# Tracing both score matmuls of a pair of token tiles ahead of VectorE's reads of the scores

## The chip, the cores and the metric

The kernel runs on one core of one Trainium2 chip. The metric is device time in microseconds (us) of one execution, from the first instruction to the last with what the launch adds around them. Engines are named as the profile names them: PE is TensorE's matmuls, PEld its weight loads, DVE is VectorE, ACT is ScalarE, POOL is GpSimd, and SP (SyncE) issues most of the DMAs.

## What is computed

The reference is one inference step of a two-layer decoder trunk: one layer of dilated-window attention (three groups of eight heads), one RG-LRU recurrent layer. There is a prompt of 1024 tokens and, beside it, eight sequences with eight new tokens each that attend to caches in HBM ("decode" below). For the prompt the part that the change touches is, per head:

```python
s = jnp.einsum('brnqhd,brnkhd->brnhqk', qb, kk) * (HEAD_DIM ** -0.5) + bias
lse = jax.nn.logsumexp(s, axis=-1)
p = jnp.exp(s - lse[..., None])
o = jnp.einsum('brnhqk,brnkhd->brnqhd', p, vv)
```

A block of 128 queries sees its own block of 128 keys and, in the groups with window 128 and 512, the block before it.

## The kernel before

All of it is fp32. The weight matmuls split each operand into a high and a low part and run three matmuls for one (lines 132, 133, 134; lines 140 and 141 for the eight sequences), each with 384 columns.

**Stages.** After a start of some 60 us, `attention_phase` runs 24 heads in the group order 1, 2, 0. A head has four quarters. Each quarter makes Q, K and V of two token tiles (`qkv_head`), normalises Q and K and transposes them on TensorE through the PSUM tile `ptq` (line 486), from which ACT copies QT (line 487) and ACT or DVE copies KT (lines 489, 491). Then it takes one attention pair from a queue that is three quarters behind (`next_att`, `att_part`, `att_pair`). From head 8 on, pieces of the decode of the caches are put between the quarters (`background`): cache tiles `kv` are loaded by SP, multiplied on POOL, DVE or ACT (lines 793, 841, 836, 829) and summed on DVE and ACT (lines 803, 798, 846), and two matmuls at line 856 close each decode. After the heads come the output projection and the recurrent layer, in which there are no pairs.

**One pair.** `att_pair` works on two token tiles, t = 0 and 1. The scores of both go into the two halves of one PSUM tile `ps_s` (line 322); there is one such buffer. DVE reads a tile's scores, adds the bias, writes `s_sb` and takes the row's extreme into `ob` (line 323, and a second small instruction that reads the accumulator); ACT takes the exponential (line 325). TensorE transposes the result into the PSUM tile `pt` (line 329), which uses the same single buffer as `ptq`. A copy to `pT` (line 94 or 92), the product with V (line 336) and a copy of the result follow. In the last group the result tile is `o3`, freed by the store `GTd<-o` and filled by loads `o<-Od`.

**What sets the order.** The program is traced in the order of the Python code. A scheduler then gives each engine its own list, which that engine executes strictly in order, and puts independent work (the weight matmuls above all) between dependent steps. Dependencies are kept by whole tiles: in the code before, the score matmul of t = 1 writes the tile that DVE's read of t = 0 reads, so it waits for that read although the halves differ.

Of the kernel before, what the change touches and what calls it, by code (L numbers as in the profile page):

```python
# [74 lines left out]
class Trunk:  # L75
# [231 lines left out]
    def att_pair(self, g, h, j, QT, KT, V, bt, ob):  # L307

        nc = self.nc
        kbs = []  # L310
        for t in range(2):
            i = 2 * j + t
            prev = [[i - 1], [i - 4], []][g]
            kbs.append([q for q in prev if q >= 0] + [i])
        ps = self.ps_s.tile([128, 2, 256], F32, name="ps_s", tag="s")
        pt = self.ps_t.tile([128, 4, 128], F32, name="pt", tag="t")
        po = self.ps_o.tile([128, 2, 132], F32, name="ps_o", tag="o")
        sb = self.p_a.tile([128, 2, 256], F32, name="s_sb", tag="s_sb", bufs=2)
        for t, kb in enumerate(kbs):
            nk = 128 * len(kb)  # L320
            kv = KT[:, kb[0], :] if len(kb) == 1 else KT[:, kb[0]:kb[1] + 1:kb[1] - kb[0], :]
            nc.tensor.matmul(ps[:, t, :nk], lhsT=QT[:, 2 * j + t, :], rhs=kv, start=True, stop=True)  # L322
            nc.vector.tensor_tensor_reduce(out=sb[:, t, :nk], in0=ps[:, t, :nk], in1=bt[:, 256 - nk:], scale=-1.0,  # L323
                                           scalar=3e38, op0=OP.add, op1=OP.min, accum_out=ob[:, t, 129:130])
            nc.scalar.activation(sb[:, t, :nk], sb[:, t, :nk], AF.Exp, bias=ob[:, t, 129:130], scale=-1.0)
        n = 0
        for t, kb in enumerate(kbs):
            for q in range(len(kb)):
                nc.tensor.transpose(pt[:, n, :], sb[:, t, 128 * q:128 * q + 128], self.ident)  # L329
                n += 1  # L330
        pT = self.p_a.tile([128, 4, 128], F32, name="pT", tag="pT", bufs=2)
        self.evac(pT[:, :n], pt[:, :n])
        n = 0
        for t, kb in enumerate(kbs):
            for q, b in enumerate(kb):
                nc.tensor.matmul(po[:, t, :129], lhsT=pT[:, n, :], rhs=V[:, b, :129],  # L336
                                 start=(q == 0), stop=(q == len(kb) - 1))
                n += 1
        self.evac(ob[:, :, :129], po[:, :, :129])
# [954 lines left out]
```

## Time and profile before

| | before |
|---|---|
| three runs, us | 1994.94, 1998.83, 1994.72 (median 1994.94) |
| profiled execution, us | 1996.83 |
| its span, first to last instruction, us | 1994.90 |
| busy, us | PE 1823.5, PEld 1748.5, DVE 1182.4, ACT 978.4, POOL 647.2 |

The page shows shares over the whole span. Because the stages have different limits, the rows below are mostly from single stretches: heads without decode (60 to 430 us), the first decode (430 to 804), the change to the last group and the second decode (804 to 1165), and heads with little decode (1165 to 1460). "a <- b: total, times, longest" in a list of waits means that a stood idle until b was done.

### The profile page before, as it was taken

To read this page: it belongs to the slowest core of one execution; us is meant where nothing else is said; L and a number is where in the kernel's file an instruction comes from. 1 tells how busy PE (TensorE), PEld (TensorE's weight loads), DVE (VectorE), ACT (ScalarE), POOL (GpSimd) and SP (SyncE) were. 2 spreads that over 40 slices of the span, in tenths; PEclk is the share of its full clock that TensorE was granted. 3 is DMA by queue.
4 is the path that set the end of the run, shared out by engine and by line. 5 is a ranking of instruction groups with operands and counts; after the bars stand their busy time and mean duration, and the time that the engine had idled before them with its cause. 6 is when DMAs were issued, how large, how long until landed. Compare 5 with 4: busy or idle time off the path is not lost.

```text
span 1994.9 us, 31531 instructions
## 1 busy us (share of the span) xinstructions
PE 1823.5 (91%) x11152; PEld 1748.5 (88%) x11152; DVE 1182.4 (59%) x2339; ACT 978.4 (49%) x3025; POOL 647.2 (32%) x606
## 2 busy tenths in 40 slices
PE   7999999978888767978887799999999999999998
PEld 7999999978888666977877689999999899999998
DVE  6334333459874999546658755455566667767721
ACT  5544444638776666442234445455423346666510
POOL 4101111247673998239746521020100000001300
PEclk9999999989999887988998899999999999999999
DMA  6655657556766656546756654454575256643231
GB/s 203 193 184 186 197 160 224 161 166 200 208 191 181 183 155 183 146 146 220 222 173 190 212 166 137 161 160 120 182 257 176 83 195 218 215 155 118 83 122 62
DMA packets 261518, 344.01 MB, mean 172 GB/s; under 512 B 19644, under 2 KB 229888, under 8 KB 259312
## 3 DMA queue, kind: packets, MB, share of 16 engines
q1 hardware_dynamic: 253540, 228.38, 39.2%
q10 hardware_dynamic: 7820, 113.61, 16.3%
q8 instruction: 88, 1.44, 0.3%
q14 instruction: 70, 0.57, 0.1%
HBM read 296.20 MB, written 157.93 MB: 228 GB/s over the span
## 4 chain that ended last, share of the span: by engine, by line
PE 47%; DMA 17%; DVE 12%; POOL 8%; ACT 7%; issue 6%; SPq 2%; ACTq 0%; DVEq 0%; POOLq 0%
PE ps_g L134 8%; PE ps_g L133 8%; PE ps_g L132 8%; POOL pr L841 4%; DMA kv<-in_cache_kv_w_dram 4%; DMA wraw<-in_rnn_w_in_dram 3%; DMA wraw<-in_attn_w_in_dram 3%; PE ps_o L336 2%; PE ps_s L322 2%; PE ps_g L1180 2%; PE ps_g L1179 2%; PE ps_g L1178 2%; POOL pr L793 2%; DVE xn L475 1%; PE ps_g L1053 1%
## 5 line engine op out<-in xcount | busy, mean ns | idle before, releaser
L132 PE MATMUL ps_g<-w,xt 128*128 128x384 f32 (+1 forms) x1920 | 668.6, 351 | 19.6 <-DVE th L400 12.2
L133 PE MATMUL ps_g<-w,xt 128*128 128x384 f32 (+1 forms) x1920 | 665.0, 347 | 3.0 <-DVE w L99 1.7
L134 PE MATMUL ps_g<-w,xt 128*128 128x384 f32 (+1 forms) x1920 | 663.8, 346 | 0.0
L132 PEld LDWEIGHTS ps_g<-w,xt 128*128 128x128 f32 x1920 | 371.9, 194 | 25.9 <-DVE th L400 13.8
L133 PEld LDWEIGHTS ps_g<-w,xt 128*128 128x128 f32 x1920 | 372.2, 194 | 7.6 <-POOL w L118 2.1
L134 PEld LDWEIGHTS ps_g<-w,xt 128*128 128x128 f32 x1920 | 371.6, 194 | 1.7
L164 POOL TENSOR_TENSOR rs<-ms,mhalf 128x4 f32<-128x4 f32 (+2 forms) x138 | 138.3, 1004 | 624.4 <-DVE ms L162 607.1
L841 POOL TENSOR_TENSOR pr<-kv,ds 128x512 f32<-128x512 f32 x116 | 182.9, 1604 | 45.1 <-DVE acc L846 17.6
L793 POOL TENSOR_TENSOR pr<-kv,dq 128x512 f32<-128x512 f32 x118 | 168.0, 1453 | 87.0 <-DMA dq<-sd 42.3
L846 DVE TENSOR_TENSOR acc<-acc,pr 128x1024 f32<-128x1024 f32 x89 | 139.7, 1590 | 11.2 <-POOL pr L841 10.9
L323 DVE CUSTOM_DVE_ANT_0 s_sb<-ps_s,bias 128x128 f32<-128x128 f32 (+1 forms) x192 | 66.4, 346 | 118.3 <-PE ps_s L322 94.1
L322 PE MATMUL ps_s<-KT,QT 128*128 128x128 f32 (+1 forms) x384 | 99.1, 341 | 37.7 <-DVE o_sb L323 25.1
L462 ACT COPY xn<-ps_g 128x256 f32<-128x256 f32 x192 | 72.1, 375 | 120.3 <-PE ps_g L134 104.4
L466 ACT ACTIVATE sqj<-xn 128x128 bf16<-128x128 f32 x384 | 121.2, 316 | 10.4 <-issue 5.2
L99 DVE TENSOR_TENSOR w<-wraw,w 128x768 fp32r<-128x768 f32 (+1 forms) x88 | 83.5, 952 | 63.7 <-ACT w L98 63.3
L98 ACT CAST w<-wraw 128x768 fp32r<-128x768 f32 (+1 forms) x88 | 69.3, 804 | 100.4 <-DMA wraw<-in_attn_w_in_dram 51.0
L836 ACT ACTIVATE pr<-kv,ds 128x128 f32<-128x128 f32 x248 | 76.8, 391 | 72.5 <-DVE acc L846 37.8
L94 DVE COPY pT<-pt 128x256 f32<-128x256 f32 (+2 forms) x96 | 52.0, 541 | 97.0 <-PE pt L329 96.5
L803 DVE TENSOR_REDUCE ds<-pr 128x8 f32<-128x1024 f32 x73 | 88.1, 1213 | 33.1 <-POOL pr L793 33.0
L475 DVE SCALAR_TENSOR_TENSOR xn<-xn,rs,kg 128x128 f32<-128x128 f32 x192 | 94.2, 530 | 22.3 <-POOL rs L164 22.2
L322 PEld LDWEIGHTS ps_s<-KT,QT 128*128 128x128 f32 x384 | 67.3, 198 | 45.6 <-DVE o_sb L323 30.2
L118 POOL TENSOR_TENSOR w<-wraw,w 128x768 fp32r<-128x768 f32 x44 | 87.3, 1993 | 58.6 <-ACT w L117 58.5
(259 smaller groups left out, 3793.3 us busy)
## 6 DMA issues: line engine op xcount, KB each, us to landing
out_dram<-in_cache_kv_w_dram ACTq DMA_DIRECT2D x32, 2032.0 KB
wraw<-in_attn_w_in_dram SPq DMA_DIRECT2D x208, 192.0 KB
kv<-in_cache_kv_w_dram SPq DMA_DIRECT2D x144, 256.0 KB
kv<-in_cache_kv_w_dram SPq DMA_DIRECT2D x64, 512.0 KB
out_dram<-in_cache_kv_w_dram ACTq DMA_DIRECT2D x16, 2016.0 KB
wraw<-in_rnn_w_in_dram SPq DMA_DIRECT2D x20, 512.0 KB
Od<-o_sb SPq DMA_DIRECT2D x64, 130.0 KB
o<-Od SPq DMA_DIRECT2D x32, 260.0 KB
```

The costliest lines, as they stand in the source:

```text
L118: nc.gpsimd.tensor_tensor(out=lo, in0=r, in1=hi.bitcast(F32), op=OP.subtract)
L132: nc.tensor.matmul(ps, lhsT=st_hi(k), rhs=w[:, 0, i, :width], start=(k == 0), stop=False)
L133: nc.tensor.matmul(ps, lhsT=st_hi(k), rhs=w[:, 1, i, :width], start=False, stop=False)
L134: nc.tensor.matmul(ps, lhsT=st_lo(k), rhs=w[:, 0, i, :width], start=False, stop=(k == n - 1))
L164: nc.gpsimd.tensor_tensor(out=rs[:np_, :n], in0=ms[:np_, :n], in1=self.mhalf[:np_, :n], op=OP.pow)
L322: nc.tensor.matmul(ps[:, t, :nk], lhsT=QT[:, 2 * j + t, :], rhs=kv, start=True, stop=True)
L466: nc.scalar.activation(junk, xn[:, y, t], AF.Square, accum_out=ss[:, t, y:y + 1])
L475: nc.vector.scalar_tensor_tensor(xn[:, 1, t], xn[:, 1, t], rs[:, 2 * t + 1:2 * t + 2], self.kg, op0=OP.mult, op1=OP.mult)
L793: (nc.vector if way == 'D' else nc.gpsimd).tensor_tensor(out=pr[c], in0=kt[c], in1=q[:, tq, c[2]].unsqueeze(1).to_broadcast(list(pr[c].sha ...
L803: nc.vector.tensor_reduce(out=s[:, tq, hs, i + m], in_=pr[:, m, c[2]].rearrange("p (h d) -> p h d", d=128), axis=AX.X, op=OP.add)
L841: nc.gpsimd.tensor_tensor(out=dst[:, m, c[2]].rearrange("p (h d) -> p h d", d=128), in0=vt[:, m, c[2]].rearrange("p (h d) -> p h d", d=128 ...
L846: nc.vector.tensor_tensor(out=acc[a], in0=acc[a], in1=dst[c], op=OP.add)
```

## The change

The loop over the two tiles is split in two: the first loop holds the two score matmuls, the second one the reads and the exponentials. Nothing is computed differently. Lines below the cut move down by two (323 becomes 325, 329 becomes 331, 336 becomes 338, 486 becomes 488, 856 becomes 858).

```diff
             nc.tensor.matmul(ps[:, t, :nk], lhsT=QT[:, 2 * j + t, :], rhs=kv, start=True, stop=True)
+        for t, kb in enumerate(kbs):
+            nk = 128 * len(kb)
             nc.vector.tensor_tensor_reduce(out=sb[:, t, :nk], in0=ps[:, t, :nk], in1=bt[:, 256 - nk:], scale=-1.0,
```

How the lists of the engines change is shown at three places. In these rows x2 means two equal instructions, and the square brackets name what the instruction waits for by its engine (or DMA queue), not by its line.

TensorE in the first group of heads, before: the second score matmul of a pair (its first, with the same wait, stands 20 rows ahead).

```order
L134 MATMUL ps_g<-w,xt 128x384
L336 MATMUL ps_o<-V,pT 128x129 [waits DVE_49]
L336 MATMUL ps_o<-V,pT 128x129
L486 MATMUL ptq<-ident,xn 128x128 [waits PE_49]
L486 MATMUL ptq<-ident,xn 128x128 x3
L322 MATMUL ps_s<-KT,QT 128x256 [waits DVE_49]
L132 MATMUL ps_g<-w,xt 128x384
L133 MATMUL ps_g<-w,xt 128x384
```

The same pair on TensorE, after:

```order
L132 MATMUL ps_g<-w,xt 128x384
L133 MATMUL ps_g<-w,xt 128x384
L134 MATMUL ps_g<-w,xt 128x384
L322 MATMUL ps_s<-KT,QT 128x256 x2
L132 MATMUL ps_g<-w,xt 128x384
L133 MATMUL ps_g<-w,xt 128x384
L338 MATMUL ps_o<-V,pT 128x129 [waits DVE_49]
L338 MATMUL ps_o<-V,pT 128x129
```

The second score matmul now stands right behind the first and waits for nothing; the place behind the transposes of `xn`, at which TensorE waited for DVE, is gone.

DVE at a pair of the first group, before (ISA is the read of the scores, the row below it the read of its accumulator):

```order
L323 ISA s_sb,o_sb<-ps_s,bias 128x256 [waits PE_49]
L323 ISA o_sb 128x1
L162 TENSOR_SCALAR ms<-ss 128x4 [waits DVE_49,Activation_49]
L473 TENSOR_TENSOR xn<-xn,rs 128x256 [waits DMAHW5_49,Pool_49]
L475 SCALAR_TENSOR_TENSOR xn<-xn,rs,kg 128x128 x2
L491 COPY KT<-ptq 128x256 [waits Activation_49]
L323 ISA s_sb,o_sb<-ps_s,bias 128x256 [waits PE_49]
L323 ISA o_sb 128x1
L94 COPY pT<-pt 128x512 [waits DVE_49,PE_49]
```

The same stretch of DVE's list, after:

```order
L325 ISA s_sb,o_sb<-ps_s,bias 128x256 [waits DMAHW0_49,PE_49]
L325 ISA o_sb 128x1
L325 ISA s_sb,o_sb<-ps_s,bias 128x256
L325 ISA o_sb 128x1
L162 TENSOR_SCALAR ms<-ss 128x4 [waits DVE_49,Activation_49]
L475 TENSOR_TENSOR xn<-xn,rs 128x256 [waits Pool_49]
L477 SCALAR_TENSOR_TENSOR xn<-xn,rs,kg 128x128 x2
L493 COPY KT<-ptq 128x256 [waits Activation_49]
L94 COPY pT<-pt 128x512 [waits DVE_49,PE_49]
```

Both reads stand together ahead of the normalisation of the next quarter, and the second has no wait of its own.

TensorE at the end of the second decode, before (`pdo` closes the decode, `acc` is its sum):

```order
L132 MATMUL ps_g<-w,xt 128x384
L856 MATMUL pdo<-acc,ind_130 64x512 [waits DVE_49]
L133 MATMUL ps_g<-w,xt 128x384
L134 MATMUL ps_g<-w,xt 128x384
L322 MATMUL ps_s<-KT,QT 128x256 [waits DVE_49]
L329 MATMUL pt<-ident,s_sb 128x128 [waits PE_49,Activation_49]
L329 MATMUL pt<-ident,s_sb 128x128 x3
L132 MATMUL ps_g<-w,xt 128x384 [waits Activation_49]
```

The same place, after:

```order
L133 MATMUL ps_g<-w,xt 128x384
L134 MATMUL ps_g<-w,xt 128x384
L858 MATMUL pdo<-acc,ind_130 64x512 [waits DVE_49]
L331 MATMUL pt<-ident,s_sb 128x128 [waits PE_49,Activation_49]
L331 MATMUL pt<-ident,s_sb 128x128 x3
L322 MATMUL ps_s<-KT,QT 128x256 x2
L132 MATMUL ps_g<-w,xt 128x384 [waits Activation_49]
L133 MATMUL ps_g<-w,xt 128x384
```

The transposes of the pair ahead still stand behind 4416 weight matmuls counted from the program's start, as before, but the waiting score matmul ahead of them is gone and the second close of the decode stands before them.

## Rows read from the trace of the kernel before

**Rows 1.** The page: busy time by engine, and the chain that ended last.

```profile
PE 1823.5 (91%) x11152; PEld 1748.5 (88%) x11152; DVE 1182.4 (59%) x2339; ACT 978.4 (49%) x3025; POOL 647.2 (32%) x606
...
PE 47%; DMA 17%; DVE 12%; POOL 8%; ACT 7%; issue 6%; SPq 2%; ACTq 0%; DVEq 0%; POOLq 0%
```

**Rows 2.** Stretches: from:to, length, busy us of PE, PEld, DVE, ACT, POOL, clock, DMA.

```profile
60.00:430.00 370.00, 360.69 (x2206) 357.08 (x2205) 132.57 (x398) 173.33 (x586) 52.47 (x54) 0.99 0.60 187
430.00:645.00 215.00, 185.63 (x1054) 175.55 (x1053) 162.18 (x240) 160.35 (x760) 141.41 (x118) 0.96 0.68 192
645.00:804.00 159.00, 114.56 (x556) 107.29 (x554) 150.93 (x153) 98.17 (x346) 145.88 (x90) 0.83 0.63 171
804.00:1000.00 196.00, 170.89 (x930) 163.59 (x930) 108.23 (x186) 70.34 (x198) 105.71 (x85) 0.90 0.59 186
1000.00:1165.00 165.00, 130.17 (x668) 120.47 (x669) 122.13 (x235) 67.56 (x225) 88.71 (x67) 0.90 0.61 192
1165.00:1460.00 295.00, 293.94 (x1960) 286.42 (x1959) 158.78 (x543) 144.68 (x469) 43.76 (x58) 1.00 0.50 157
```

**Rows 3.** The page's costliest groups: busy, mean ns | idle before, its main releaser.

```profile
L322 PE MATMUL ps_s<-KT,QT 128*128 128x128 f32 (+1 forms) x384 | 99.1, 341 | 37.7 <-DVE o_sb L323 25.1
```

**Rows 4.** Waits of PE, 430 to 645 us: total, times, longest.

```profile
PE ps_s L322 <- DVE o_sb L323: 16.5, 13, 3.6
PE pt L329 <- ACT KT L489: 8.1, 9, 1.8
```

**Rows 5.** Waits of DVE in the same stretch; one of the three that name PE.

```profile
DVE s_sb L323 <- PE ps_s L322: 0.6, 1, 0.6
```

**Rows 6.** The chain that ended last in the same stretch, shares by line.

```profile
by line: issue 13.0%; DMA wraw<-in_attn_w_in_dram 11.5%; ACT junk L798 10.6%; DVE pr L793 10.1%; POOL pr L793 8.0%; DMA kv<-in_cache_kv_w_dram 7.5%; DVE ds L803 6.9%; POOL rs L164 3.1%; DVE xn L475 3.0%; SPq L809 2.7%; ACT sqj L466 1.9%; DV
```

**Rows 7.** Waits of ACT in the same stretch.

```profile
ACT s_sb L325 <- DVE o_sb L323: 13.2, 14, 2.0
```

**Rows 8.** Waits of DVE, 645 to 804 us.

```profile
DVE acc L846 <- POOL pr L841: 6.0, 7, 2.0
DVE s_sb L323 <- PE ps_s L322: 2.7, 1, 2.7
```

**Rows 9.** PE in order of time from 686 us: start, us, instruction, [idle before <- releaser].

```profile
686.10 0.79 PE L322 MATMUL ps_s<-KT,QT 128*128 128x128 f32 x2 [6.73 <-DVE o_sb L323]
...
688.29 0.52 PE L132 MATMUL ps_g<-w,xt 128*128 128x384 f32 x1
688.61 0.52 PE L133 MATMUL ps_g<-w,xt 128*128 128x384 f32 x1
```

**Rows 10.** PE in order of time at the end of the first decode.

```profile
800.17 0.34 PE L132 MATMUL ps_g<-w,xt 128*128 128x384 f32 x1
800.34 0.34 PE L133 MATMUL ps_g<-w,xt 128*128 128x384 f32 x1
...
804.27 1.07 PE L856 MATMUL pdo<-acc,ind 128*64 128x512 f32 x2 [0.75 <-DVE acc L846]
```

**Rows 11.** Waits of PE, 1000 to 1165 us.

```profile
PE ps_s L322 <- DVE o L323: 11.6, 6, 2.7
...
PE pt L329 <- ACT KT L489: 6.3, 3, 5.1
```

**Rows 12.** PE in order of time at the end of the second decode.

```profile
1154.38 0.80 PE L322 MATMUL ps_s<-KT,QT 128*128 128x128 f32 x2 [2.70 <-DVE o L323]
...
1158.06 1.07 PE L856 MATMUL pdo<-acc,ind 128*64 128x512 f32 x2
...
1161.26 0.66 PE L329 MATMUL pt<-ident,s_sb 128*128 128x128 f32 x4 [0.36 <-ACT KT L489]
```

**Rows 13.** DVE in order of time at the same place.

```profile
1155.19 1.59 DVE L846 TENSOR_TENSOR acc<-acc,pr 128x1024 f32<-128x1024 f32 x1
...
1159.84 0.29 DVE L323 CUSTOM_DVE_ANT_0 s_sb<-ps_s,bias 128x128 f32<-128x128 f32 x1 [2.77 <-DMA GTd<-o]
```

**Rows 14.** Waits of PE, 1165 to 1460 us.

```profile
PE ps_s L322 <- DVE o L323: 0.4, 1, 0.4
```

## The prediction

> **What bounds the kernel now.** I read the page first. TensorE is busy 91% of the span, its weight loads 88%, DVE 59%; yet the chain that ended last runs through TensorE for only 47% of the time and through DMA, DVE, POOL and ACT for 44% [rows 1]. So the kernel has stages with different limits, and I cut the span at the marks of the decode [rows 2]. From 60 to 430 us and from 1165 to 1460 us TensorE is the limit (360.69 of 370 and 293.94 of 295 us busy). From 430 to 804 us the first decode loads everything else: POOL and DVE are busy 145.88 and 150.93 of 159 us in the second half of it, TensorE 114.56. From 804 to 1165 us it is mixed.
>
> The line that the change touches is the score matmul, L322. TensorE sat idle 37.7 us before it, and the releaser is DVE's read L323 [rows 3]: the second matmul of a pair waits for the read of the first. In the early heads, 60 to 430 us, no wait of that kind is listed at all. They lie at 430 to 645 us (16.5 us in 13 waits) [rows 4], at 645 to 804 us (8.6 us, of which 6.73 us is one wait [rows 9]), at 1000 to 1165 us (11.6 us in 6) [rows 11], with 0.4 us after that [rows 14]; 0.6 us is left for the rest. The reader is to see that every one of them falls into a stretch in which the other engines hardly wait for TensorE. From 430 to 645 us DVE's waits name TensorE three times, 1.5 us in all, and the row for the scores is 0.6 us [rows 5]; the chain there names weight and cache loads, the decode's sums and products and no TensorE line among its large shares [rows 6]. From 645 to 804 us DVE's largest wait is for POOL, 6.0 us, and one for the scores, 2.7 us [rows 8].
>
> **The change, part by part.** *Work:* the instructions are the same ones. TensorE executes the score matmuls in the same number and form, 99.1 us in all [rows 3], DVE the same reads. In the order 93 of 96 pairs now have the two matmuls next to each other, where 22, 28 and 39 instructions lay between them on average in the three groups. Zero.
>
> *First read.* It now waits for both matmuls. TensorE needs at most 0.70 to 0.80 us for one [rows 9, 12], and the two reads then run without a second wait. The cover is the distance to the transposes L329: 42, 107 and 107 TensorE instructions on average in the three groups now. At 0.175 us each (start to start at 2.4 GHz, 800.17 to 800.34 [rows 10]) that is 7 us in the first group and 19 us in the others. Zero in the first and last stretch. If the cover went, it would cost up to 0.8 us a pair.
>
> *430 to 645 us.* From above the whole 16.5 us come back; from below nothing, since nobody waits for TensorE. I take it near the lower end, because of [rows 5, 6]. One thing is on the path there: ACT stands 13.2 us in 14 waits for the reads [rows 7], and it holds the decode's sums (10.6% of the chain [rows 6]). ACT's list now has the two exponentials side by side, so two places to wait become one. Half of 13.2 us is 6.6, and ACT's lines that the row shows are 12.5% of the chain, so 0.8 us are gained.
>
> *645 to 804 us.* DVE is busy 150.93 of 159 us [rows 2]. The wait of 6.73 us ended with DVE's read [rows 9], which stands behind decode sums in DVE's list; in the new list it stands behind the same ones, and TensorE will wait elsewhere. From above 2.7 us [rows 8], from below zero. I take zero.
>
> *End of the first decode.* L856 waits for DVE's last sum and is served at 804.27 us after 0.75 us of idle [rows 10]. Ahead of it stood 3133 weight matmuls in the program, now 3125; its first instruction moved from 3133 to 3104. Eight fewer done, when the sum ends at the same time, cost 8 x 0.175 = 1.4 us; 28 would cost 4.9 us. Behind it TensorE is the busiest again (170.89 of 196 us [rows 2]), so I let this count in full. From below zero, if the sum ends earlier. I take 1.4 us lost.
>
> *1000 to 1165 us.* From here TensorE works without idle time to 1460 us [rows 2, 14], so what it gains by 1161 us counts in full. From above: 11.6 us [rows 11] and the slow clock behind the long ones. That price: after the 6.73 us of idle the weight matmuls start 0.32 us apart (688.29 to 688.61 [rows 9]) where they start 0.175 us apart otherwise; ten or so at 0.145 us are 1.5 us. The waits here are shorter, 2.7 us at most, so I give half of the six such a tail: 4.5 us. Together 16.1 us. From below: at 1161.26 us TensorE waits at L329 for the KT copy [rows 12]. ACT made that copy behind the exponential of the read at 1159.84 us, which itself waited for a store from the result tile [rows 13]. This step stands behind 4416 weight matmuls in both orders. If the store lands when it did, TensorE is let go there as before, and only 0.3 us are won. L856 ahead of it needs the sum that ends at 1156.8 us [rows 13], now behind 4402 instead of 4414. The row nearest to the question is that at 1161.26, so I stay close to the lower end: 3.0 us gained.
>
> The 0.4 us after 1165 us [rows 14] are gained. Sum: -0.8 - 0 + 1.4 - 3.0 - 0.4 = -2.8 us. Against the profiled execution (1996.83 us, a span of 1994.90 and 1.93 around it) that is 1994.0; the median of the three runs is 1.89 us lower, 1994.94, and gives **1992 us**. This is 0.14% less than before; a measurement of this kernel can tell about 0.2%, 4 us, from no change.
>
> **The rivals.** *A, TensorE's lag is carried along.* TensorE's idle time at 1000 to 1165 us comes back nearly in full, since a TensorE that is ahead lets QT, KT and the projections be ready earlier and so pulls DVE and ACT along. For it: after 1165 us TensorE alone is the limit. Against it: the store behind which the read at 1159.84 us stood [rows 13]. Time: 1994.94 - 16.1 - 0.8 + 1.4 - 0.4 = 1979 us.
>
> *B, all waits are on the path.* 37.7 us, and a tail of 1.5 us of slow clock behind ten of them (half of the 21 in [rows 4, 9, 11] and their stretches), 53 us: 1942 us; the idle time alone gives 1957. For it: TensorE's busy shares [rows 1]. Against it: the shares of the chain in the same rows.
> The Trainium skill points this way: "Perfetto Trace Analysis", section "Identifying the Most-Contended Engine", picks the engine to optimise by occupancy, for TensorE by its weight loads, which at 88% against 59% of DVE is TensorE, and its next section has one close the gaps on that engine. By that rule the price is that of B. The stretches [rows 2] speak against it: where the gaps lie, DVE and POOL are as busy or busier.
>
> *C, slower: ACT holds the KT copy longer.* ACT's list now has both exponentials in a row ahead of the QT and KT copies of the next quarter. When DVE is late, ACT stands for the second read as well (0.29 us for one [rows 13]) and works on a second exponential, some 0.8 us in all as an estimate from that row, before it copies KT, and the transposes share that PSUM buffer. TensorE already waits for that copy, 8.1 us in 9 waits at 430 to 645 us [rows 4] and 6.3 us in 3 at 1000 to 1165 us [rows 11]. Twelve times 0.8 are 9.6 us: 1992 + 9.6 = 2002 us. It decides where TensorE reaches L329 before the copy, which is where the waits removed had held it back until now.
>
> *D, the edit is undone by the scheduler.* The order excludes it: the pairs are adjacent.
>
> **How the numbers follow.** The forecast (own range 1988 to 1999) 0.40, A 0.28, B 0.06, C 0.26. A stands for times from 1973 to 1988, by how much of the 16.1 us and of the 16.5 us earlier is kept. The range that leaves out 2 in 10 drops B, the far end of A and the far end of C: 1974 to 2004 us. Faster by over 0.2% (under 1991): A, B and the low part of the forecast, 0.28 + 0.06 + 0.07 = 0.41. Slower by over 0.2% (over 1999): 0.26 of C less 0.02 that falls inside, 0.24. The same: 0.35.
>
> **What would show it.** Right: the wait L322 <- L323 is gone from all stretches; heads up to 430 us take as long as before; DVE's and POOL's busy time from 645 to 804 us is the same and L856 is served at about 804 us; the idle time of TensorE turns up before L329, L336 and L856; at 1161 us the profile has moved by under 5 us. A is right if that step comes 10 us earlier or more. C is right if waits of L331 for KT copies and of ACT for the reads grow. Wrong altogether: a gain or loss before 430 us, or a decode that ends more than 5 us off, which would mean that the small moves in the lists of SP and DVE, which I priced at nothing, weigh more than the waits.

## The result, and the profile after

The changed kernel takes **2014.87 us** (median of 6 runs, 2003.26 to 2021.08) beside 1994.83 us for the kernel before in the same session: a ratio of 1.0092, 95% interval 1.0072 to 1.0111. It is slower by 0.9%, where 1992 us was predicted. The profiled execution took 2019.06 us, its span is 2017.3 us at a mean granted clock of 0.954, where before had 1994.9 us at 0.961.

The page of after: busy time by engine, then one row of its costliest groups (busy, mean ns | idle before, releaser). In after every line behind L322 has moved down by 2, so L323, L329, L336, L841, L846 and L856 of before are L325, L331, L338, L843, L848 and L858.

```profile
PE 1819.7 (90%) x11152; PEld 1751.8 (87%) x11152; DVE 1179.3 (58%) x2339; ACT 976.5 (48%) x3025; POOL 638.9 (32%) x606
...
L338 PE MATMUL ps_o<-V,pT 128*128 128x129 f32 x560 | 87.2, 292 | 59.7 <-DVE pT L94 59.7
```

Every engine executes as many instructions as in [rows 1]. What grew is the idle time of TensorE, span less busy: from 171.4 to 197.6 us. The view by line, all groups of TensorE (busy, mean ns | idle before, releasers), first of before (three lines that [rows 3] does not hold), then of after:

```profile
L132 PE MATMUL ps_g<-w,xt 128*128 128x384 f32 (+1 forms) x1920 | 668.6, 351 | 19.6 <-DVE th L400 12.2 <-ACT w L98 3.3 <-ACT V L463 2.7
...
L336 PE MATMUL ps_o<-V,pT 128*128 128x129 f32 x560 | 83.7, 285 | 16.1 <-DVE pT L94 16.1
...
L329 PE MATMUL pt<-ident,s_sb 128*128 128x128 f32 x280 | 54.7, 290 | 39.3 <-ACT KT L489 19.7 <-DVE KT L491 18.9 <-ACT s_sb L325 0.8
```

```profile
L132 PE MATMUL ps_g<-w,xt 128*128 128x384 f32 (+1 forms) x1920 | 669.1, 352 | 33.7 <-ACT V L465 12.5 <-DVE th L402 8.8 <-ACT xt L250 4.3
...
L322 PE MATMUL ps_s<-KT,QT 128*128 128x128 f32 (+1 forms) x384 | 82.5, 339 | 10.5 <-DVE o L325 10.5
...
L331 PE MATMUL pt<-ident,s_sb 128*128 128x128 f32 x280 | 49.7, 282 | 26.2 <-ACT KT L491 15.0 <-DVE KT L493 7.8 <-ACT s_sb L327 3.3
```

Add the three attention lines: scores, transposes and value matmuls waited 37.7 + 39.3 + 16.1 = 93.1 us before and 10.5 + 26.2 + 59.7 = 96.4 us after. The wait at the scores was taken away and came back, a little larger, at the value matmul L338, which waits for VectorE's copy of the transposed weights, pT. On top of that the projections L132 wait 14.1 us longer, mostly for ScalarE's copies of V.

The stretches. The third one ends at the matmul that [rows 10] shows at 804.27 us and that stands at 816.13 us now, the last one at the second decode's second close (1175.59 us, 1164.71 in before); [rows 2] has 645 to 804 and 1000 to 1165. Length, busy us of PE, PEld, DVE, ACT and POOL, clock.

```profile
60.00:430.00 370.00, 360.58 (x2210) 357.47 (x2209) 126.97 (x397) 171.02 (x580) 50.65 (x54) 0.99 0.58 186
430.00:645.00 215.00, 178.29 (x1010) 171.70 (x1009) 169.04 (x235) 156.64 (x749) 134.18 (x114) 0.93 0.66 190
645.00:816.00 171.00, 119.39 (x595) 112.20 (x593) 152.59 (x169) 104.44 (x362) 149.39 (x94) 0.80 0.61 166
...
1012.00:1176.00 164.00, 123.36 (x644) 115.30 (x645) 116.67 (x230) 64.36 (x212) 85.25 (x65) 0.90 0.61 190
```

Up to 430 us nothing has changed. From 430 to 645 us TensorE gets through 1010 instructions where it had 1054, at a granted clock of 0.93 instead of 0.96. From 645 us to the end of the first decode VectorE has about the same busy time as before (152.59 us, 150.93 in before), in 171 us instead of 159. The waits of TensorE there, and in the next stretch:

```profile
PE ps_o L338 <- DVE pT L94: 24.1, 8, 7.9
PE pt L331 <- ACT KT L491: 10.8, 6, 4.0
```

```profile
PE ps_o L338 <- DVE pT L94: 24.4, 5, 9.4
PE ps_g L132 <- ACT V L465: 11.0, 3, 4.7
```

Against [rows 4] the 16.5 us in 13 waits, 3.6 the longest, have become 24.1 us in 8, 7.9 the longest: fewer and longer. TensorE in order of time at the two ends of decode, which answer to [rows 10] and [rows 12]:

```profile
808.45 1.97 PE L858 MATMUL pdo<-acc,ind 128*64 128x512 f32 x2 [4.42 <-DVE acc L848]
...
810.84 0.52 PE L141 MATMUL ps_gs<-w,xs 128*128 128x384 f32 x1
811.16 0.52 PE L140 MATMUL ps_gs<-w,xs 128*128 128x384 f32 x1
...
816.13 1.07 PE L858 MATMUL pdo<-acc,ind 128*64 128x512 f32 x2
```

```profile
1169.03 1.07 PE L858 MATMUL pdo<-acc,ind 128*64 128x512 f32 x2 [2.80 <-DVE acc L848]
...
1177.12 0.66 PE L331 MATMUL pt<-ident,s_sb 128*128 128x128 f32 x4 [0.46 <-ACT KT L491]
```

The matmul of [rows 10] at 804.27 us, which had 3133 weight matmuls ahead of it and now has 3125, is the one at 816.13 us: 11.9 us later. The one at 808.45 us, for which TensorE stands 4.42 us, is the close ahead of it, which was at 802.45 us. VectorE's sums of the first decode are late from the start: the first ends at 657.2 us (648.1 in before), the last at 812.37 (804.22). After the wait TensorE's instructions start 0.32 us apart for 2.4 us (810.84 to 811.16 in the rows), the lower level of its clock. The second decode's first close is 11.0 us later, and the step that was at 1161.26 us is at 1177.12. Behind it TensorE works nearly without a pause, as before, so these 15.9 us stay to the end; 6.5 more are lost after that.

Where do they arise? A head leaves a mark in the trace, GpSimd's MEMSET of its V tile; a head is said here to begin at that mark. Two marks of before, then the same two of after:

```profile
766.33 0.11 POOL L444 MEMSET V<- 128x8 f32 x1
...
821.77 0.12 POOL L444 MEMSET V<- 128x8 f32 x1 [2.95 <-PE ps_o L336]
```

```profile
765.37 0.11 POOL L446 MEMSET V<- 128x8 f32 x1
...
831.54 0.12 POOL L446 MEMSET V<- 128x8 f32 x1 [4.10 <-PE ps_o L338]
```

At the marks of 562.60 and 616.99 us the kernel after was 9.0 and 11.2 us behind, and at 765.37 us it was level again (1.0 us ahead): what the early waits cost had been made up. (The run e4 below shows the same: 11.3 us behind at 617.1, 2.5 ahead at 763.8, 8.2 behind at 830.0.) The head from there on takes 10.6 us longer, and this loss stays (the next mark is at 868.51 us, 857.04 in before). Its stretch, before and after:

```profile
766.30:821.80 55.50, 45.82 (x230) 41.09 (x229) 47.20 (x69) 27.61 (x101) 37.88 (x29) 0.88 0.60 175
```

```profile
765.40:831.50 66.10, 48.21 (x235) 42.15 (x234) 54.52 (x77) 31.55 (x111) 44.75 (x30) 0.79 0.62 172
```

TensorE stands 17.9 us in it instead of 9.7, of which the value matmul's waits for pT are 11.8 us (5.6 in before) and the close's wait for the decode's sum is 4.4 us (0.8), and its granted clock is 0.79 instead of 0.88.

### The profile page after: what moved, and what is told of

It is laid out like the page before. It is cut to its first block, busy times and chain, and to the rows that moved or that the text cites. A ratio compares the mean times of both kernels' runs of the same rounds, so it can differ in the third digit from the quotient of the medians.

```text
span 2017.3 us, 31518 instructions
## 1 busy us (share of the span) xinstructions
PE 1819.7 (90%) x11152; PEld 1751.8 (87%) x11152; DVE 1179.3 (58%) x2339; ACT 976.5 (48%) x3025; POOL 638.9 (32%) x606
## 4 chain that ended last, share of the span: by engine, by line
PE 34%; DMA 11%; DVE 9%; issue 5%; POOL 5%; ACT 3%; SPq 1%; ACTq 0%; DVEq 0%; POOLq 0%
PE ps_g L132 4%; PE ps_g L133 4%; PE ps_g L134 4%; DMA kv<-in_cache_kv_w_dram 3%; PE ps_g L1053 3%; PE ps_g L1055 3%; PE ps_g L1054 3%; DVE acc L848 2%; DMA wraw<-in_rnn_w_in_dram 2%; POOL pr L843 2%; PE ps_g L1182 2%; PE ps_g L1180 2%; PE ps_g L1181 2%; DMA wraw<-in_attn_w_in_dram 2%; DMA gd<-th 1%
## 5 line engine op out<-in xcount | busy, mean ns | idle before, releaser
L132 PE MATMUL ps_g<-w,xt 128*128 128x384 f32 (+1 forms) x1920 | 669.1, 352 | 33.7 <-ACT V L465 12.5
L133 PE MATMUL ps_g<-w,xt 128*128 128x384 f32 (+1 forms) x1920 | 661.3, 345 | 8.3 <-DVE w L99 4.7
L132 PEld LDWEIGHTS ps_g<-w,xt 128*128 128x128 f32 x1920 | 372.4, 194 | 39.7 <-ACT V L465 14.0
L133 PEld LDWEIGHTS ps_g<-w,xt 128*128 128x128 f32 x1920 | 373.0, 194 | 11.7 <-DVE w L99 5.1
L164 POOL TENSOR_TENSOR rs<-ms,mhalf 128x4 f32<-128x4 f32 (+2 forms) x138 | 139.0, 1010 | 664.1 <-DVE ms L162 611.4
L843 POOL TENSOR_TENSOR pr<-kv,ds 128x512 f32<-128x512 f32 x116 | 178.4, 1564 | 47.5 <-DMA kv<-in_cache_kv_w_dram 22.9
L848 DVE TENSOR_TENSOR acc<-acc,pr 128x1024 f32<-128x1024 f32 x89 | 133.1, 1518 | 25.3 <-POOL pr L843 20.2
L338 PE MATMUL ps_o<-V,pT 128*128 128x129 f32 x560 | 87.2, 292 | 59.7 <-DVE pT L94 59.7
L338 PEld LDWEIGHTS ps_o<-V,pT 128*128 128x128 f32 x560 | 79.7, 203 | 65.6 <-DVE pT L94 49.8
L468 ACT ACTIVATE sqj<-xn 128x128 bf16<-128x128 f32 x384 | 121.6, 317 | 11.2 <-issue 5.3
L325 DVE CUSTOM_DVE_ANT_0 s_sb<-ps_s,bias 128x128 f32<-128x128 f32 (+1 forms) x192 | 59.6, 346 | 111.1 <-PE ps_s L322 72.7
L477 DVE SCALAR_TENSOR_TENSOR xn<-xn,rs,kg 128x128 f32<-128x128 f32 x192 | 93.7, 528 | 17.9 <-POOL rs L164 17.9
```

The costliest lines, as they stand in the source:

```text
L132: nc.tensor.matmul(ps, lhsT=st_hi(k), rhs=w[:, 0, i, :width], start=(k == 0), stop=False)
L133: nc.tensor.matmul(ps, lhsT=st_hi(k), rhs=w[:, 1, i, :width], start=False, stop=False)
L164: nc.gpsimd.tensor_tensor(out=rs[:np_, :n], in0=ms[:np_, :n], in1=self.mhalf[:np_, :n], op=OP.pow)
L468: nc.scalar.activation(junk, xn[:, y, t], AF.Square, accum_out=ss[:, t, y:y + 1])
L477: nc.vector.scalar_tensor_tensor(xn[:, 1, t], xn[:, 1, t], rs[:, 2 * t + 1:2 * t + 2], self.kg, op0=OP.mult, op1=OP.mult)
L843: nc.gpsimd.tensor_tensor(out=dst[:, m, c[2]].rearrange("p (h d) -> p h d", d=128), in0=vt[:, m, c[2]].rearrange("p (h d) -> p h d", d=128 ...
```

## Why the pT copy is late

VectorE runs its list in order, and the copy stands behind operations of the decode. VectorE in order of time before the first long wait (start, us, operation), then GpSimd in the same microseconds, then TensorE:

```profile
451.86 8.13 DVE L508 SCALAR_TENSOR_TENSOR sraw<-sraw,rs,qgs 64x128 f32<-64x128 f32 x1
459.92 0.33 DVE L508 SCALAR_TENSOR_TENSOR sraw<-sraw,rs,kg 64x128 f32<-64x128 f32 x1
460.18 1.21 DVE L805 TENSOR_REDUCE ds<-pr 128x8 f32<-128x1024 f32 x1
461.31 0.41 DVE L94 COPY pT<-pt 128x256 f32<-128x256 f32 x1
```

```profile
451.33 3.63 POOL L118 TENSOR_TENSOR w<-wraw,w 128x768 fp32r<-128x768 f32 x2
454.93 4.91 POOL L795 TENSOR_TENSOR pr<-kv,dq 128x512 f32<-128x512 f32 x4
```

```profile
461.77 1.23 PE L338 MATMUL ps_o<-V,pT 128*128 128x129 f32 x4 [7.66 <-DVE pT L94]
```

An operation that takes 0.33 us the next time took 8.13 us: it lasted until GpSimd's six operations in a row had ended. In before the two operations of that line took 0.80 and 1.94 us at this place (at 451.01 and 451.74 us). The second long wait has another cause, which goes through SyncE's queue. SyncE's store and load, VectorE and TensorE:

```profile
577.23 0.39 SPq L484 DMA_DIRECT2D out_dram<-xn  x1
577.72 2.98 SPq L611 DMA_DIRECT2D kv<-in_cache_kv_w_dram  x1
```

```profile
574.51 2.69 DVE L477 SCALAR_TENSOR_TENSOR xn<-xn,rs,kg 128x128 f32<-128x128 f32 x2 [0.90 <-POOL rs L164]
...
583.65 1.23 DVE L795 TENSOR_TENSOR pr<-kv,dq 128x1024 f32<-128x1024 f32 x1 [4.90 <-DMA kv<-in_cache_kv_w_dram]
584.91 1.22 DVE L805 TENSOR_REDUCE ds<-pr 128x8 f32<-128x1024 f32 x1
586.05 0.41 DVE L94 COPY pT<-pt 128x256 f32<-128x256 f32 x1
```

```profile
586.52 1.23 PE L338 MATMUL ps_o<-V,pT 128*128 128x129 f32 x4 [7.94 <-DVE pT L94]
```

The store of xn waits for VectorE until 577.2 us; the cache load stands behind that store; VectorE's product waits 4.90 us for the load; the copy stands two operations behind the product; TensorE waits 7.94 us for the copy. These two waits are among those whose time was made up by 765 us. The third and longest is in the head that loses the 10.6 us, and it is the plain case: the copy stands behind three sums of the decode, the first of which waited for GpSimd.

```profile
779.57 5.18 DVE L848 TENSOR_TENSOR acc<-acc,pr 128x1024 f32<-128x1024 f32 x3 [0.94 <-POOL pr L843]
784.67 0.41 DVE L94 COPY pT<-pt 128x256 f32<-128x256 f32 x1
```

```profile
785.23 1.20 PE L338 MATMUL ps_o<-V,pT 128*128 128x129 f32 x4 [9.38 <-DVE pT L94]
```

Between the last transpose of a pair and its first value matmul TensorE's list holds on average 24 to 28 instructions by group in both kernels, 4.2 to 4.9 us at 0.175 us each. That is all the cover the copy has.

## The experiments

All were timed beside the kernel before. Ratios are to before, with 95% intervals. One caution on single profiles: e13, e14 and e18 have the lists of before up to about 860 us, and the head that begins at 857.04 us in the profile of before begins 1.7 to 4.3 us earlier in theirs. A shift of under 5 us in one profile is not read.

| run | kernel | median us | ratio, interval | clock |
|---|---|---|---|---|
| after | both matmuls first | 2014.87 | 1.0092, 1.0072-1.0111 | 0.954 |
| e1 | before, two score tiles | 2066.38 | 1.0351, 1.0319-1.0383 | 0.944 |
| e2 | before, pT on ScalarE | 1998.57 | 1.0019, 1.0002-1.0036 | 0.961 |
| e3 | after, pT on ScalarE | 2004.39 | 1.0030, 1.0017-1.0044 | 0.955 |
| e4 | first in group 2 only | 2011.72 | 1.0073, 1.0054-1.0093 | 0.952 |
| e5 | after, late value matmuls | 2005.18 | 1.0033, 1.0011-1.0056 | 0.959 |
| e6 | before, late value matmuls | 2002.97 | 1.0028, 1.0008-1.0047 | 0.963 |
| e9 | after, late in group 2 only | 2005.10 | 1.0044, 1.0026-1.0062 | 0.962 |
| e10 | before, late in group 2 only | 1998.09 | 1.0011, 0.9999-1.0024 | 0.962 |
| e11 | first in groups 1 and 0 | 2011.00 | 1.0069, 1.0043-1.0094 | 0.961 |
| e12 | before, tile 1 ahead of tile 0 | 1998.88 | 1.0017, 1.0001-1.0033 | 0.956 |
| e13 | before, query transposes apart | 2000.07 | 1.0021, 1.0005-1.0038 | 0.968 |
| e14 | first in the last two heads only | 1997.21 | 1.0007, 0.9991-1.0022 | 0.964 |
| e15 | e9, group 0 as before | 2013.40 | 1.0077, 1.0049-1.0106 | 0.955 |
| e16 | first in group 1 only | 2010.96 | 1.0069, 1.0043-1.0094 | 0.962 |
| e17 | tile 1 first, group 1 only | 1997.78 | 1.0003, 0.9988-1.0019 | 0.961 |
| e18 | first in group 0 only | 2000.07 | 1.0022, 0.9998-1.0046 | 0.962 |

**e1: the wait taken away with the order of the Python code as before.**

```
-ps = self.ps_s.tile([128, 2, 256], F32, name="ps_s", tag="s")
+ps = [self.ps_s.tile([128, 256], F32, name="ps_s", tag="s"),
+      self.ps_d.tile([128, 256], F32, name="ps_s", tag="d")]
```

> The code order of before; only the place of the second token tile's scores changes: it gets a PSUM tile of its own in the bank of tag 'd', so the second score matmul no longer has to wait for VectorE's read of the first. Theory Q (queue: TensorE, no longer held at the second score matmul, comes to the value matmul of the pair before VectorE has done the pT copy, which stands in VectorE's list behind decode operations): L322's wait for VectorE falls from 37.7 us to under 10, the value matmul's wait for the pT copy grows from 16.1 us to 40-60, time 2005-2020 us. Theory O (order: the changed code order shuffles every engine's list and SyncE's loads, and that alone costs the 0.9%; the freed wait is harmless): time 1985-1998 us, pT waits stay near 16 us.

The decode's softmax uses tag "d" as well, from its first transpose on (635 us in before). Ahead of it, from 430 to 605 us, TensorE's waits are these, first of before, then of e1:

```profile
PE ps_s L322 <- DVE o_sb L323: 12.5, 11, 1.9
...
PE ps_o L336 <- DVE pT L94: 1.8, 3, 0.7
```

```profile
PE ps_o L336 <- DVE pT L94: 21.0, 10, 4.9
```

Over the whole span the value matmuls wait 41.7 us for pT, as theory Q expected, and the time, 2066.38 us, is what neither theory expected. The code keeps its order in e1, but the lists do not: in the order of execution, behind the first decode operation, e1 has 910 of VectorE's 1881 instructions elsewhere than before, the kernel after 721. So e1 alone does not separate the freed matmul from a new list order. All runs together do: the value matmuls wait 59.7, 53.5 and 41.7 us for pT in the three that free the scores of group 2 and leave the copy and the value matmuls as they were (after, e4, e1), and 12.4 to 20.1 us in the eight that leave that wait as it was (before, e11 to e14, e16 to e18), though some of these displace over 400 of VectorE's instructions. It is the freed matmul that sends TensorE into the wait for pT. The time of e1 says nothing on the change: some 32 us of delay arise between the heads that begin at 613 and 697 us in e1 (606 and 658 in before), where scores and softmax share the bank, and most of it is made up by 830 us; some 47 us arise between 1279 and 1438 us. That part was not taken apart.

**e4: the change in group 2 alone**, the eight heads beside the first decode.

```
+if g == 2:
+    for t, kb in enumerate(kbs):
+        score(t, kb)
 for t, kb in enumerate(kbs):
+    if not (g == 2):
+        score(t, kb)
```

> Both score matmuls first only in the eight heads of group 2, the code of before in groups 1 and 0. Those heads run from about 430 to 800-970 us, where the first cache decode's operations (1.2 and 2 us each) stand in VectorE's list. Theory Q: the start of the heads up to 430 us is unmoved, 40 us or more of waits at the value matmul between 430 and 806 us, the head that began at 857 us begins 8-13 us later, and the end is 2003-2010 us. Theory O: loss or gain anywhere, and no more likely here; 1985-2015 us.

Waits of TensorE in e4, 430 to 645 us (L343 is the value matmul):

```profile
PE ps_o L343 <- DVE pT L94: 25.1, 8, 7.9
PE pt L336 <- ACT KT L496: 7.8, 5, 3.9
```

The pattern of after is there, wait for wait, and the head that began at 857 us begins 9.9 us later (11.5 in after). Group 2 alone is enough for 0.73%; the time, 2011.72 us, is 2 us above what theory Q expected.

**e2, e3: the copy moved to ScalarE** (and the pair's output copy to VectorE), in before and after.

```
-self.evac(pT[:, :n], pt[:, :n])
+nc.scalar.copy(pT[:, :n], pt[:, :n])
```

> before, with the pT copy always on ScalarE and the copy of the pair's output (ps_o) on VectorE instead of the other way round; the control for e3. Theory Q: before had only 16.1 us of waits for the pT copy, 5.6 the longest, so 1985-2000 us. Theory O: any change of list order may cost about 1%, 1985-2015 us.

> after, with the pT copy always on ScalarE and the copy of the pair's output on VectorE. Theory Q: the 59.7 us in which the value matmul waits for VectorE's pT copy are gone or below 20, since ScalarE's list holds no decode operation of 1.2 us or more there; time falls by 10-25 us to 1990-2005 us, and against e2 the change is no longer slower (within 0.3%). Theory O: the copy's engine does not matter, e3 stays 0.6-1.2% above e2, 2005-2025 us. The rival that ScalarE's two adjacent exponentials hold something up: e3 grows above 2020 us.

The cost falls from 0.92% to 0.30%, and the control stands at 0.19%: with the copy off VectorE the change costs 0.1%, inside the intervals. The wait did not vanish, against what was expected. In e3 the waiters for pT include:

```profile
PEld ps_o L338: 31.3, 13
```

The matmuls behind these loads wait 30.2 us in 13 (59.7 in 17 in after), now for ScalarE; 14.9 us of it lie between 430 and 806 us, where after has 48.5. The lists change in these two runs as well, so the lower cost is not shown to come from the copy alone.

**e5, e6, e9, e10: more cover for the copy.** The value matmuls of a pair come behind the transposes of the next pair, so mostly 60 to 76 instructions stand in between instead of 24. e5 and e6 do it in groups 1 and 2, e9 and e10 in group 2 only.

```
+last = nc.tensor.transpose(...)      # the next pair's
+self.flush(last)                     # issue_after(last): value matmuls of the pair before
-for t, kb in enumerate(kbs): ... nc.tensor.matmul(po[:, t, :129], ...)
```

> after, with the value matmuls of a pair (groups 1 and 2) held back until the transposes of the next pair have been issued: in TensorE's list 66 to 68 instructions stand between a pair's last transpose and its first value matmul instead of 24 to 26, about 11.7 us of cover for VectorE's pT copy instead of 4.3 at the 0.175 us per instruction of the trace. Theory Q (too little cover for a copy that is late in VectorE's list): the 48 us of waits at the value matmul between 430 and 806 us shrink to under 10, a few of them turn up at the next pair's transposes; time 1985-2003 us, so at least 12 us under after. Theory O (list order in general): 2000-2030 us. Theory V (VectorE's own pace bounds the decode stretch, whatever TensorE waits at): the waits turn up elsewhere in full, and the time stays at 2008-2020 us.

> before, with the same edit as e5: the control. Its waits for the pT copy are 16.1 us in all. Theory Q: 1980-1997 us, within 0.5% of before, and e5 lies within 0.4% of it on either side. Theory V: as before, 1990-2000 us, and e5 stays 0.7% or more above it.

e5 costs 0.33%, its control e6 0.28%: with the cover the change costs nothing that can be measured beside its control. Between 430 and 806 us the value matmuls no longer wait for pT (48.5 us in after); 16.4 us of waits for it stand before L506 instead. The time is 2 us above what theory Q expected, and the lists changed here too. Waits in e5, 430 to 645 us; L506 are the transposes of Q and K, which share the PSUM buffer with pT:

```profile
PE pt L330 <- ACT KT L509: 9.6, 6, 2.7
PE ptq L506 <- DVE pT L94: 6.7, 4, 3.2
```

> after, with the value matmuls held back behind the next pair's transposes in group 2 alone (the eight heads beside the first cache decode; 68 instructions of cover there, 24 in groups 1 and 0 as in after). e5 lost 10 us by 457 us, in heads that have no decode beside them, and was at +3 us at 1171 us. Theory Q: without the loss in group 1 the time is 1987-2000 us, at least 15 us under after and no slower than before. Theory V: 2008-2020 us.

> before, with the same edit as e9: the control. Theory Q: L322's wait (25 us between 430 and 806 us) stays, so e10 is within 0.4% of e9 on either side, 1987-2000 us. Theory V: e9 at least 0.6% above e10.

Here the expectation failed: e9 is 0.3% above e10. Its trace, the same operation as above on VectorE and TensorE's waits from 430 to 645 us:

```profile
451.54 8.14 DVE L526 SCALAR_TENSOR_TENSOR sraw<-sraw,rs,qgs 64x128 f32<-64x128 f32 x1
```

```profile
PE ptq L506 <- DVE pT L94: 19.5, 7, 7.6
```

The 8-us hold is there in after, e4, e9 and e15 (8.13 to 8.16 us each). In these four, and in no other run with decode beside the heads, VectorE's last product of the first decode starts at 615.8 to 617.1 us; in before it starts at 603.8, in the others between 602.5 and 608.8. The hold alone does not explain it: e3 has one of 8.22 us at 507.72 and e5 one of 6.90 us at 454.55, and their last products start at 608.7 and 603.9. So cover for group 2 alone does not do what cover for groups 1 and 2 does in e5; why was not settled.

**e7, e8: no decode beside the heads.** All decode steps are issued behind the last head in both kernels.

> before, with every cache decode issued only after the last attention head (none of its operations stands beside the heads); all is still computed, so the time is longer by some of the decode's 600 us. The pair for e8. Theories Q and V: L322's wait for VectorE between 430 and 1165 us, 36.7 us in before, falls below 5.

> after, with the same edit as e7. Theories Q and V: without decode operations in VectorE's list no long wait for the pT copy arises, and e8 is within 0.2% of e7. Theory O (any change of order costs about 1%): the two differ by 8 us or more, either way.

2367.23 and 2380.84 us, 13.6 us or 0.6% apart: more than theories Q and V allow, and as much as theory O asked for. But the difference does not lie in the heads, whose waits are nearly as Q and V expected (5.0 us at L322 in e7, 1.6 us at the value matmul in e8 between 430 and 1165 us): the last score matmul starts at 1235.7 and at 1234.5 us, the last value matmul at 1253.5 and at 1247.5. It comes behind them: the lone decode, which was tied to the last head's Q copy, comes to its first softmax transpose 13.6 us later (1396.5 and 1410.1 us). So without decode beside them the heads lose nothing; on the total the pair decides nothing between Q and O.

**e11, e16, e18, e12, e17: the other groups, and order as such.** e11 is e4 with the condition turned round, e16 and e18 have it for group 1 and for group 0. e12 and e17 move no wait: they trace tile 1 ahead of tile 0.

```
-for t, kb in enumerate(kbs):
+for t, kb in ((1, kbs[1]), (0, kbs[0])):     # e17: in group 1 only
```

> The complement of e4: both score matmuls first in groups 1 and 0, the code of before in group 2. Theory Q: the loss of after is 0.92%, that of e4 0.73%, so here 0.0 to 0.4%, 1994-2004 us, with less than 20 us of waits at the value matmul before 1165 us. Theory O: about as much as after, 2008-2020 us, as it reorders the lists in twice as many heads.

> A measure of what a change of order alone does: before, with the scores of the pair's second token tile traced ahead of the first one's (matmul, read, exponential of t=1, then of t=0; the wait between the two matmuls stays). Theory Q: within 0.4% of before, 1989-2003 us, since no wait is moved. Theory O: 0.5-1.2% off before, either way.

> Both score matmuls first only in group 1, whose heads (60 to 430 us) have no decode beside them. Theories Q and T: within 0.2% of before, 1991-1999 us, heads up to 442 us at most 5 us earlier. Theory O: 0.4% or more off before, either way, though no wait is moved.

> before, with the second token tile's scores traced ahead of the first one's (matmul, read, exponential of t=1, then of t=0) in group 1 alone; no wait is taken away. Theory O (a change of order in group 1 carries on into the lists of the decode stretches and costs by that): 0.4-0.8% above before, 2003-2011 us, as e16. Theory M (it is the two matmuls standing first): within 0.25% of before, 1990-2000 us.

> Both score matmuls first in group 0 alone (from about 970 us on). By the difference of e11 and e16 (both 0.69%) it costs nothing: 0.0-0.25%, 1993-2000 us. Theory O: 0.4% or more, since VectorE's list from 1000 us on is as much reordered as in after. Unmoved up to 900 us in either case, but for a few microseconds between executions.

e11 and e16 were expected near zero and cost 0.69% each. Group 1's own heads lose nothing (the mark behind them is at 442.4 us, at 446.7 in before). The loss comes later, in heads whose code is that of before, and without the waits of after. In e16 the first decode's last sum ends when it did (804.4 us); the heads of 857.0 and 1168.1 us begin 5.1 and 10.2 us late. Busy time by stretch in e16:

```profile
60.00:430.00 370.00, 360.01 (x2205) 356.91 (x2205) 126.55 (x397) 170.88 (x582) 50.83 (x54) 0.99 0.59 186
430.00:645.00 215.00, 181.17 (x1042) 170.86 (x1041) 166.99 (x241) 158.87 (x760) 140.13 (x116) 0.98 0.68 192
...
1012.00:1176.00 164.00, 126.25 (x643) 114.17 (x643) 113.92 (x232) 66.84 (x223) 86.45 (x65) 0.90 0.62 194
```

TensorE stands 15.9 us longer than before in all, spread over L133 (7.6 us more), L132 (5.8), the merge transposes L417 (5.8) and others; the mean granted clock is that of before (0.962, 0.961). As their code is the same, what can reach the later heads is where the scheduler puts their operations. By a comparison of the two programs' lists, behind the first decode operation 253 of 1882 instructions of VectorE's list and 119 of 868 of SyncE's stand elsewhere than in before. e17 moves 81 and 30 there and costs nothing; but e12 moves 416 and 100, e18 402 and 103, and they cost 0.17% and 0.22%. So the amount of reordering does not set the loss, and which move does it in e16 stays open; nor is it shown that a move in the lists does.

**e13, e14, e15: a theory that fell.** In after and e11 the query transposes of the last decode piece stand 86 instructions apart in TensorE's list, 9 in before, and that piece ends 31 to 36 us later (1508.4 us in before, 1539.5 in e11, 1544.1 in after).

```
e13: +with self.tc.high_priority():   # around the transposes of qr in decode0
e14:  score(t, kb) first if g == 0 and h >= 6
e15:  e9 with score(t, kb) first only if g > 0
```

> before, with the transposes of the decode pieces' queries (qr) in a high-priority block; in TensorE's list the last piece's two then stand 97 instructions apart instead of 9. Theory T (the last decode piece, started late, ends late and holds up the end): unmoved up to about 1300 us, the last decode piece ends 15-30 us later (1508 us in before), and from the last head's start to the end 622-627 us pass where before took 615.7; time 2001-2007 us. Theory O: no such link, the stretch stays within 3 us of 615.7, time within 0.3% of before.

> Both score matmuls first only in the last two heads of group 0 (86 instructions between the two query transposes of the last decode piece, as in after); all other heads as in before. Theory T: unmoved up to 1321 us, then the last decode piece ends at 1530-1545 us instead of 1508, and 6-10 us are lost behind 1379 us: 2001-2007 us. Theory O: within 0.3% of before.

> e9 with the change taken out of group 0: both score matmuls first in groups 1 and 2, the value matmuls of group 2 behind the next pair's transposes, the code of before in group 0 (query transposes 9 apart). Theories Q and T together: no loss is left, 1990-2000 us, at least 4 us under e9 and within 0.2% of e10. If it stays at e9's 2005 us, T does not hold.

e13 puts them 97 apart and costs 0.21%, e14 86 apart and 0.07%, not the expected 0.3 to 0.6%, and the last piece ends only 1.5 and 9.5 us later than in before; e15 with 9 apart is no better than e9 but worse, 0.77%. The place of these transposes is not the cause. Where the last 6.5 us of after are lost stays open.

No version beats the kernel before; the nearest, e17, is equal to it.

## Why the prediction was wrong, step by step

- *The wait at L322 goes; heads up to 430 us are unmoved.* Right up to 806 us, where 25.1 us became nothing. Over the span 37.7 us became 10.5, of which 6.6 us are one wait between 1012 and 1176 us. Up to 430 us TensorE is busy 360.58 of 370 us (360.69).
- *TensorE's waits beside the decode are cover and will turn up elsewhere.* Right in the sum, 93.1 and 96.4 us at the three attention lines, and wrong in what it was taken to mean. The idle time was named as turning up before L329, L336 and L856, and the forecast let it do so at no cost. **This is the step that failed.** It held up to 765 us, where the kernel after had lost nothing; the next head took 10.6 us longer, with 11.8 us of waits at the value matmul (5.6 in before) and 4.4 at the close (0.8). At L336 nothing was priced: neither that the copy's cover is some 24 instructions, 4.2 us, where the distance between the two score matmuls was 22 to 39, nor that the copy stands behind decode operations of 1.2 and 2 us in VectorE's list.
- *430 to 645 us: a gain of 0.8 us.* TensorE lost 7.3 us of busy time there (185.63 to 178.29), and made it up by 765 us. The gain was to come from ScalarE having one place to wait instead of two; its waits for the reads went from 13.2 us in 14 [rows 7] to 12.8 in 7. The places halved, the time did not.
- *645 to 804 us: zero, and 1.4 us at the end of the first decode.* These are the terms that were mis-sized most. The matmul of [rows 10] is 11.9 us late, the decode's last sum 8.2 us; the eight fewer weight matmuls ahead of it were counted rightly (3125), but the sum did not end at the same time. (The other bound's 28 are 29 by its own counts, 3133 and 3104.) VectorE's busy time was rightly seen as unchanged; it needed 171 us for it instead of 159, as its list holds different things ahead of the decode's steps, which was not priced.
- *1000 to 1165 us: a gain of 3.0 us, at most 5 either way.* The step is 15.9 us later instead, but 11.5 us of that were there at the mark of 868.51 us. The first decode's sum, 8.2 us late, already is the sign that the prediction gave for being wrong altogether: more than 5 us off, with small moves in the lists of VectorE and SyncE weighing more than the waits.
- *Rival C, the KT copy held up by ScalarE's two exponentials.* The side was right, the mechanism was not. Waits for KT copies at the transposes fell from 38.6 us (19.7 + 18.9) to 22.8 (15.0 + 7.8); only from 430 to 645 us did those for ScalarE's copies grow, from 8.1 us [rows 4] to 10.8. e3, which puts every pT copy on ScalarE, is not above 2020 us as that rival expected but at 2004.
- *Rivals A and B.* TensorE's lag was not carried along; it grew. Against B the prediction held that where the gaps lie DVE and POOL are as busy or busier. By its own [rows 2] that is so from 645 to 804 us alone; from 430 to 645 and from 1000 to 1165 us, where most of the waits lay, TensorE is the busiest (185.63 and 130.17 us). So the trace does not speak against the rules cited from the Trainium skill ("Perfetto Trace Analysis", sections "Identifying the Most-Contended Engine" and "Optimization Strategy"), to optimise the most-contended engine first and to find the gaps on it. TensorE's gaps were not closed but moved, and with 26.2 us more idle time of TensorE the profiled span is 22.3 us longer. What was wrong is B's price, that a gap closed at one line is a gap gone.
- *The range.* 1974 to 2004 us left out 2015. Its slow end was one mechanism of 9.6 us. What a new order of the lists may cost, 0.0 to 0.2% in e12, e13, e14 and e17 and perhaps the 0.7% of e16, was excluded without a row.

What is shown: the wait moved to the value matmul because TensorE was freed (after, e4 and e1 against the eight runs that leave the wait), and the time that is lost for good up to 860 us is lost in a head where this wait is the largest. With more cover for the copy or on another engine the cost falls by about two thirds (e5, e3). What is argued and not shown: that the moved wait is the cause of the 0.9%. The first decode itself runs 8 to 9 us late in after, from before 657 us on, and it does not in e5 and e16; no run separates a late decode from a late TensorE. e5 and e3 change the lists as well, and cover for group 2 alone (e9, e15) did not help as it does in e5. Open too is the loss of e16, and so why the groups do not add up (0.69%, 0.73% and 0.22% alone, 0.92% together).

## What to carry to other kernels

Here a wait on an engine that was not the limit of its stretch was not removed by taking away its place: it moved to the next place where the two lists meet. What it costs there depends on whether the time can be made up: the early waits were, the one ahead of the decode's end was not. Before such a change, go to that place, count the instructions that cover it and lay beside them what the other engine's list holds ahead of the awaited operation. And where a scheduler writes the lists, an edit in one phase reorders the phases behind it, and one that keeps the order of the code can reorder more (e1): test it group by group, with a control that moves no wait, before its effect is put down to the wait.

## What the runs showed of the hardware

A VectorE operation on two SBUF operands can be held for as long as GpSimd has operations in a row. L508 took 8.13 us from 451.86 us, until GpSimd's run of 451.33 to 459.84 us had ended, and 0.33 us the next time; the holds of 8.15 us in e4, 8.14 in e9, 8.22 in e3 and 6.90 in e5 also end 0.1 to 0.2 us behind the last of such a run. The Trainium skill has a reason ("SBUF — State Buffer", section "SBUF: two separate sides"): VectorE operations with two SBUF inputs and GpSimd operations that read SBUF lock a shared pair of ports, and the other one blocks for the whole instruction. The trace agrees that it blocks, and goes further: it was held past five instruction boundaries of GpSimd, not past one. It need not be: in before the two operations of this line took 0.80 and 1.94 us and ended 0.1 us behind the end of one GpSimd operation each (451.81 behind 451.67, 453.68 behind 453.53), with GpSimd going on. What decides between the two is not shown.
